# Two of four SwiGLU half-steps with seven half-size products per hidden tile in place of eight

## The chip, the cores and the metric

The kernel runs on one core of a Trainium2 chip, as one program. The time is the device time of the whole program in microseconds (us), the median of three runs. The engines are called TensorE (PE in the rows; PEld is its weight load), VectorE (DVE), ScalarE (ACT), GpSimd (POOL) and SyncE (SP, which only issues transfers here).

## The reference

Two layers run over a latent stream of 512 tokens and a context stream of 256 tokens, 1024 features wide, in float32. Each layer is a half-step, a mixer, and another half-step:

```python
x = x + 0.5 * mx[2] * _swiglu(_modulate(_rmsnorm(x, norm_g[l, 0]), mx[0], mx[1]),
                              ffn_w1[l, 0], ffn_w3[l, 0], ffn_w2[l, 0])
...
x = x + mx[5] * ox
...
x = x + 0.5 * mx[8] * _swiglu(_modulate(_rmsnorm(x, norm_g[l, 2]), mx[6], mx[7]),
                              ffn_w1[l, 1], ffn_w3[l, 1], ffn_w2[l, 1])

def _swiglu(h, w1, w3, w2):
    return (jax.nn.silu(h @ w1) * (h @ w3)) @ w2
```

`mx` is the latent stream's nine adaLN vectors, made from `silu(c) @ w_mod[l] + b_mod[l]`. The context stream takes the same steps with its own vectors; in the second layer it ends in the mixer, so that layer's second half-step is for the latent tokens alone. `w1` and `w3` are 1024 by 2816, `w2` is 2816 by 1024. The mixer is a projection `h @ w_in`, pooling, a retention with four heads, a convolution of 31 taps, and `@ w_out`. The output is the latent stream after a last norm.

## The kernel before

Features lie on the partitions and tokens along the free dimension. A float32 product is made exactly enough from three narrow ones: `split` (L150, L151) cuts a tile into a high part on ScalarE and a low part on VectorE, and `mm3` multiplies high by high, high by low and low by high into one bank of PSUM (L155 to L157).

`weights` gives the next 1024 columns of weights in the order of their use; it loads a block (L528) into one of six `raw` buffers, splits it, and works three blocks ahead (`LOOKAHEAD`). There are four buffers for high parts `wh` and four for low parts `wl`, so a block's split waits until TensorE has released the one four before it. All other activations lie in a pool of 66 slots of 128 by 512 values.

A half-step (`ffn`) goes through the 22 tiles of 128 hidden features in five pieces of 5, 5, 4, 4 and 4 (`PIECES`). For each tile, `up` multiplies eight tiles of `h` by `w1` and by `w3`, first for the 256 context tokens and then for the 512 latent ones; ScalarE takes the silu (L561), VectorE multiplies (L562), and `split` makes the parts of `g`. At the end of a piece come its products with `w2` (`down`), and VectorE adds them, times a gate, to the stream `x` in its slots (L599). In the last piece the squares of `x` are summed as well (L400, L401), a group's norm starts when its last tile is added, and `norm_tiles` (L474 to L480) makes the next `h`. In that last piece all the context's products come first, then all the latent ones, so one group's norm runs beside the other's products.

The adaLN vectors are made in the background by `mod_chunks`: loads of `w_mod`, multiplications on VectorE (L301, L303), and a small sum on TensorE (L319). What runs in the background is a generator; `spawn` and `poll` place its parts between TensorE's products by a clock that counts 0.000422 us for each column multiplied, and `drain` places all that is left at once:

```python
self.first = [self.spawn(self.mod_chunks(0, (2,), 4.0), 10.0)]
later = self.spawn(self.mod_chunks(0, range(3, 9), 6.0), 80.0)
...
    self.ffn(l, 0, h, both, both, both, done, begun)
    self.drain(later)
    self.decays()
```

While a mixer runs, `x` is kept in DRAM: `store_x` writes it after the norm, `load_x` reads it back before the products with `w_out`. The convolution's taps are a background task on VectorE (L745); `conv_norm`'s transposes (L845) come when all taps have been placed. The order on each engine comes from a scheduler, which takes of the ready instructions the one that comes first in the program.

## Time and profile before

| | |
|---|---|
| median of three runs | 2616.26 us (2614.4 to 2616.76) |
| span of the profiled execution | 2612.7 us |
| the median less that span | 3.6 us |
| TensorE, busy | 2580.8 us (99%) |
| VectorE, busy | 1624.4 us (62%) |
| ScalarE, busy | 722.5 us (28%) |
| DMA, mean | 104 GB/s |

The span is from the first to the last instruction of one profiled execution. For that execution there is no device time of its own, so what lies around the span is taken from the median of the runs. A busy time says how long an engine had an instruction in it; TensorE's matmuls overlap, so its share alone does not say that it is the limit.

### The profile page before, as it was taken

The page shows a single profiled execution, that of the slowest core. Times are in us where ns is not written, and L with a number is a line of the kernel's source. Part 1 is how long each engine was busy: PE and PEld are TensorE (multiplying, and loading weights), DVE is VectorE, ACT ScalarE, POOL GpSimd, SP SyncE. Part 2 cuts the span into 40 slices and gives each one's busy share as a digit, 9 for nine tenths or more (in the row PEclk, how much of TensorE's full clock was granted, in tenths as well). Part 3 has the DMA queues.
Part 4 walks back from the last instruction along what each step waited for, and adds up shares of the span by engine and source line. Part 5 has one row for each costly group of instructions (what it writes and reads, how often), then busy time and mean ns, then how long its engine had stood idle before and what let it go on. Part 6 is the DMA issues. An engine that isn't in the chain of part 4 may idle for free. (4 is left out here: it accounts for less than half of the span.)

```text
span 2612.7 us, 35462 instructions
## 1 busy us (share of the span) xinstructions
PE 2580.8 (99%) x14434; PEld 2241.5 (86%) x14434; DVE 1624.4 (62%) x3058; ACT 722.5 (28%) x1204; POOL 0.2 (0%) x4
## 2 busy tenths in 40 slices
PE   8999999999999999999999999999999999999998
PEld 4888888888898888888888888888888888888887
DVE  6776685747977777677333863645536697633335
ACT  3212112133334331212212412121223254422223
POOL 0000000000000000000000000000000000000000
PEclk9999999999999999999999999999999999999999
DMA  7343443322232134354211241433212332233331
GB/s 279 115 146 113 145 153 104 113 85 87 85 97 81 57 105 151 96 158 126 72 61 57 85 134 57 136 105 97 81 58 98 97 109 81 74 106 111 96 96 35
DMA packets 88003, 270.82 MB, mean 104 GB/s; under 512 B 10272, under 2 KB 12832, under 8 KB 87840
## 3 DMA queue, kind: packets, MB, share of 16 engines
q1 hardware_dynamic: 84768, 264.36, 32.1%
q10 hardware_dynamic: 3072, 4.20, 0.6%
q8 instruction: 113, 1.85, 0.3%
q14 instruction: 50, 0.41, 0.0%
HBM read 256.98 MB, written 7.34 MB: 101 GB/s over the span
## 5 line engine op out<-in xcount | busy, mean ns | idle before, releaser
L155 PE MATMUL up<-h,wh 128*128 128x512 f32 (+1 forms) x2496 | 852.1, 343 | 3.4 <-ACT h L476 1.7
L156 PE MATMUL up<-h,wh 128*128 128x512 f32 (+1 forms) x2496 | 853.0, 342 | 0.4 <-DVE h L478 0.2
L157 PE MATMUL up<-h,wl 128*128 128x512 f32 (+1 forms) x2496 | 849.9, 342 | 0.1
L150 ACT CAST wh<-raw 128x1024 fp32r<-128x1024 f32 (+1 forms) x348 | 344.0, 993 | 1261.7 <-PE down L156 442.2
L151 DVE TENSOR_TENSOR wl<-raw,wh 128x1024 fp32r<-128x1024 f32 (+1 forms) x348 | 398.2, 1148 | 333.1 <-ACT wh L150 318.2
L155 PEld LDWEIGHTS up<-h,wh 128*128 128x128 f32 x2496 | 472.2, 190 | 59.4 <-ACT h L476 2.0
L156 PEld LDWEIGHTS up<-h,wh 128*128 128x128 f32 x2496 | 473.0, 190 | 55.9 <-DVE h L478 1.0
L157 PEld LDWEIGHTS up<-h,wl 128*128 128x128 f32 x2496 | 472.3, 189 | 54.5 <-DVE wl L151 0.3
L155 PE MATMUL down<-g,wh 128*128 128x512 f32 (+1 forms) x1264 | 430.9, 341 | 0.0
L156 PE MATMUL down<-g,wh 128*128 128x512 f32 (+1 forms) x1264 | 430.3, 341 | 0.0
L157 PE MATMUL down<-g,wl 128*128 128x512 f32 (+1 forms) x1264 | 429.0, 339 | 0.0
L303 DVE SCALAR_TENSOR_TENSOR macc<-wm,sc,macc 128x512 f32<-128x512 f32 x462 | 319.0, 745 | 9.8 <-DMA wm<-in_w_mod_dram 9.6
L562 DVE TENSOR_TENSOR silu<-silu,up 128x512 f32<-128x512 f32 (+1 forms) x156 | 88.3, 566 | 341.1 <-PE up L157 340.7
L155 PEld LDWEIGHTS down<-g,wh 128*128 128x128 f32 x1264 | 239.7, 190 | 27.5 <-ACT g L150 0.2
L156 PEld LDWEIGHTS down<-g,wh 128*128 128x128 f32 x1264 | 239.8, 190 | 26.8 <-DVE g L151 0.6
L157 PEld LDWEIGHTS down<-g,wl 128*128 128x128 f32 x1264 | 239.3, 189 | 27.1
L599 DVE SCALAR_TENSOR_TENSOR x<-down,gate,x 128x256 f32<-128x256 f32 (+1 forms) x288 | 177.7, 621 | 136.3 <-PE down L157 134.4
L150 ACT CAST g<-silu 128x512 fp32r<-128x512 f32 (+1 forms) x156 | 81.8, 525 | 210.5 <-DVE silu L562 210.5
L745 DVE SCALAR_TENSOR_TENSOR conv<-z,dwh,conv 128x512 f32<-128x512 f32 (+1 forms) x180 | 109.8, 656 | 1.6
L151 DVE TENSOR_TENSOR g<-silu,g 128x512 fp32r<-128x512 f32 (+1 forms) x156 | 88.6, 568 | 23.7 <-ACT g L150 23.6
L561 ACT ACTIVATE silu<-up 128x512 f32<-128x512 f32 (+1 forms) x156 | 77.3, 496 | 87.0 <-PE up L157 86.7
L476 ACT ACTIVATE h<-ht,mod 128x256 fp32r<-128x256 f32 (+1 forms) x96 | 56.3, 597 | 81.5 <-DVE ht L474 81.4
(175 smaller groups left out, 2268.4 us busy)
## 6 DMA issues: line engine op xcount, KB each, us to landing
raw<-in_w_dram SPq DMA_DIRECT2D x224, 512.0 KB, 3.7
wm<-in_w_mod_dram SPq DMA_DIRECT2D x128, 512.0 KB, 3.9
raw<-in_w_dram SPq DMA_DIRECT2D x64, 320.0 KB, 3.0
raw<-in_w_feat_dram SPq DMA_DIRECT2D x36, 512.0 KB, 3.6
wm<-in_w_mod_dram SPq DMA_DIRECT2D x32, 256.0 KB, 6.0
raw<-in_w_out_dram SPq DMA_DIRECT2D x16, 512.0 KB, 4.8
xkept<-x SPq DMA_DIRECT2D x20, 256.0 KB, 2.5
x<-xkept SPq DMA_DIRECT2D x20, 256.0 KB, 6.0
```

Source lines behind the costliest of these rows:

```text
L150: self.nc.scalar.copy(hi, src)
L151: self.nc.vector.tensor_sub(lo, src, hi.bitcast(F32))
L155: nc.tensor.matmul(out, wh, xh, start=start, stop=False)
L156: nc.tensor.matmul(out, wh, xl, start=False, stop=False)
L157: nc.tensor.matmul(out, wl, xh, start=False, stop=stop)
L303: self.nc.vector.scalar_tensor_tensor(acc[v], raw, s, acc[v], op0=ALU.mult, op1=ALU.add)
L476: nc.scalar.activation(hi, t, AF.Identity, bias=sh)
L561: nc.scalar.activation(t, ps[f, 0], AF.Silu)
L562: nc.vector.tensor_mul(t, t, ps[f, 1])
L599: nc.vector.scalar_tensor_tensor(xd, ps, self.gate(l, idx, grp[0], dt), xd, op0=ALU.mult, op1=ALU.add)
L745: nc.vector.scalar_tensor_tensor(acc, src, w, acc, op0=ALU.mult, op1=ALU.add)
```

## The change

In the second half-step of the first layer and the first of the second layer (`HALVED`), the products of `h` with `w1` and `w3` are made by Strassen's scheme in Winograd's form. The 768 tokens are two halves of 384 (latent tokens 0 to 383; then latent 384 to 511 and the context), the 1024 features two halves of 512, and `w1` and `w3` of a hidden tile are the two halves of the output. Seven products of half size take the place of eight; sums and differences of the weights' halves are made for each tile on VectorE (`blocks`), those of `h` once for a half-step (`differences`, `first_difference`). The first two hidden tiles are still made the old way while the differences are made.

These half-steps go in eleven pieces of two hidden tiles. What a piece adds to the stream is no longer added on VectorE: ScalarE scales it into a slot and GpSimd issues a transfer that adds it to the stream in DRAM (`add_kept`); the stream is read back in the last tile. The first half of the products with `w_out` is added the same way in both mixers.

Besides: `PIECES` is 4, 4, 4, 4, 4, 2 in all half-steps; `h` lies in 16 rows of 768 tokens, and the other slots are 45; `raw` has five buffers; the first three adaLN vectors of the second layer are made in the first half-step and not in the second; two kinds of tiles of the mixer use other pools.

```diff
-PIECES = (5, 5, 4, 4, 4)
+PIECES = (4, 4, 4, 4, 4, 2)
...
+HALVED = ((0, 1), (1, 0))
+HK, HN, SUB = KD // 2, NT // 2, 2
+PARKED = ((0, 1), (1, 1), (0, 2), (1, 0))
...
-        self.spool = ctx.enter_context(tc.tile_pool(name="slots", bufs=66))
+        self.spool = ctx.enter_context(tc.tile_pool(name="slots", bufs=45))
+        self.rpool = ctx.enter_context(tc.tile_pool(name="rows", bufs=2 * KD))
...
+    def row(self, s, dt=F32):
+        return self.rpool.tile([P, NT], dt, tag="row", name=self.name(s))
...
+    def add_kept(self, dt, grp, ps, gate):
+        st, t0, n = grp
+        part = self.slot("xpart")[:, :n]
+        self.nc.scalar.activation(part, ps, AF.Copy, scale=gate)
+        c0 = dt * LEN[st] + t0
+        self.nc.gpsimd.dma_start(self.kept[st][:, c0 : c0 + n], part, accum_op=ALU.add)
...
-    def mod_chunks(self, l, js, pace):
...
+    def mod_chunks(self, ljs, pace):
+        nc = self.nc
+        for l, j in ljs:
...
-        if idx == 1:
-            if l < DEPTH - 1 or grp[0] == LAT:
+        if (l, idx) in PARKED:
+            if idx != 1 or l < DEPTH - 1 or grp[0] == LAT:
                 self.store_x(grp[0])
...
-        return self.wpool.tile([P, 1024], F32, tag="raw", name=self.name("raw"), bufs=6)[:, :n]
+        return self.wpool.tile([P, 1024], F32, tag="raw", name=self.name("raw"), bufs=5)[:, :n]
...
+        def halved(l, s):
+            f0 = 0
+            for npc in PIECES:
+                w2 = ins["w2"][l, s, :, f0 * D : (f0 + npc) * D].rearrange("p (d f n) -> p d f n", d=KD, f=npc)
+                for a in range(0, npc, SUB):
+                    for f in range(f0 + a, f0 + a + SUB):
+                        both = [ins["w13"][l, s, f, :, m * 1024 : (m + 1) * 1024] for m in range(2)]
+                        if f < NFIRST:
+                            yield from both
+                        else:
+                            yield both
+                    for d in range(0, KD, 4):
+                        yield w2[:, d : d + 4, a : a + SUB]
+                f0 += npc
...
+    def fetch(self, src):
+        raws = []
+        for a in src if isinstance(src, list) else [src]:
+            n = a.shape[-1] if len(a.shape) == 2 else 1024
+            raws.append(self.raw(n))
+            to = raws[-1] if len(a.shape) == 2 else raws[-1].rearrange("p (d f n) -> p d f n", d=4, f=SUB)
+            self.nc.sync.dma_start(to, a)
+        return raws
...
+        order = self.weight_order()
+        src = next(order)
+        raws = None
+        while src is not None:
+            if raws is None:
+                raws = self.fetch(src)
+            after = next(order, None)
+            early = None
+            if not isinstance(src, list):
+                if isinstance(after, list):
+                    early = self.fetch(after)
+                self.parts(raws[0])
+                yield
+            else:
+                w1, w3 = raws
+                half = slice(0, 512), slice(512, 1024)
+                b, c = self.raw(1024), self.raw(1024)
+                nc.vector.tensor_sub(b[:, half[0]], w1[:, half[0]], w3[:, half[0]])
+                nc.vector.tensor_add(c[:, half[0]], w3[:, half[0]], w3[:, half[1]])
+                self.parts(w1)
+                yield
+                nc.vector.tensor_sub(b[:, half[1]], c[:, half[0]], w1[:, half[0]])
+                self.parts(b)
+                early = self.fetch(after) if after is not None else None
+                yield
+                nc.vector.tensor_sub(c[:, half[1]], w1[:, half[1]], b[:, half[1]])
+                self.parts(c)
+                yield
+                self.parts(w3[:, half[1]])
+                yield
+            src, raws = after, early
...
+    def prepare(self, n):
+        while self.plan and len(self.ahead) < n:
+            if next(self.plan, self) is self:
+                self.plan = None
...
+    def sums(self, h, kt):
+        t = []
+        for k in (kt, kt + HK):
+            for c in (slice(0, HN), slice(HN, NT)):
+                t.append(self.slot("half")[:, :HN])
+                self.nc.vector.tensor_add(t[-1], h[0][k][:, c].bitcast(F32), h[1][k][:, c].bitcast(F32))
+        return t
...
+    def differences(self, h, T):
+        nc = self.nc
+        for kt in range(HK):
+            b11, b12, b21, b22 = self.sums(h, kt)
+            nc.vector.tensor_sub(b11, b12, b11)
+            nc.vector.tensor_sub(b12, b22, b12)
+            nc.vector.tensor_sub(b22, b22, b11)
+            nc.vector.tensor_sub(b21, b21, b22)
+            for i, t in ((3, b12), (2, b22), (4, b21)):
+                for p in range(2):
+                    T[i][p][kt] = self.slot("t", F32R)[:, :HN]
+                self.split(t, T[i][0][kt], T[i][1][kt])
+            yield 3.6
...
+    def first_difference(self, h):
+        nc = self.nc
+        a, b = slice(0, HN), slice(HN, NT)
+        for kt in range(HK):
+            t, u = (self.slot("half")[:, :HN] for _ in range(2))
+            for v, c in ((t, b), (u, a)):
+                nc.vector.tensor_add(v, h[0][kt][:, c].bitcast(F32), h[1][kt][:, c].bitcast(F32))
+            nc.vector.tensor_sub(t, t, u)
+            self.split(t, h[0][kt][:, b], h[1][kt][:, b])
...
+    def up_halved(self, f, h, T, g, load=None):
+        nc = self.nc
+        self.prepare(4)
+        wa, wb, wc, wd = (self.ahead.pop(0) for _ in range(4))
+        a, b = slice(0, HN), slice(HN, NT)
...
+            for kt in range(HK):
+                c = slice(half * 512 + kt * P, half * 512 + (kt + 1) * P)
+                self.mm3(ps, w[0][:, c], w[1][:, c], tile(0, kt), tile(1, kt), start and kt == 0, kt == HK - 1, True)
+            self.poll()
...
+        pa, pd = (self.psum("up")[:, :HN] for _ in range(2))
+        product(pa, wa, 0, of_h(0, a), True)
+        c11 = copied(pa)
+        product(pd, wb, 0, of_t(3), True)
+        p7 = copied(pd)
+        product(pa, wb, 1, of_t(2), False)
+        c21 = copied(pa)
+        if load:
+            load()
+        pb = self.psum("up")[:, :HN]
+        product(pb, wa, 1, of_h(HK, a), True)
+        nc.vector.tensor_add(c11, pb, c11)
+        nc.scalar.activation(c11, c11, AF.Silu)
+        self.prepare(1)
+        product(pa, wc, 0, of_h(0, b), False)
+        c22 = copied(pa)
+        self.prepare(2)
+        product(pd, wd, 0, of_t(4), False)
+        nc.vector.tensor_add(c21, pd, c21)
+        nc.vector.tensor_mul(c11, c11, c21)
+        grp = (LAT, 0, HN)
+        self.split(c11, self.put(g, 0, f, grp, "g0"), self.put(g, 1, f, grp, "g1"))
+        nc.vector.tensor_add(c22, c22, p7)
+        product(pa, wc, 1, of_h(HK, b), False)
+        self.prepare(3)
+        nc.scalar.activation(p7, pa, AF.Silu)
+        nc.vector.tensor_mul(p7, p7, c22)
+        for grp, c in (((CTX, 0, LC), slice(HN - LC, HN)), ((LAT, HN, LX - HN), slice(0, LX - HN))):
+            self.split(p7[:, c], self.put(g, 0, f, grp, "g0"), self.put(g, 1, f, grp, "g1"))
+        self.prepare(4)
...
+    def ffn_halved(self, l, s, h, starts, grps, ends, done):
+        nc = self.nc
+        idx = 2 * s
+        accs = {}
+        T = {i: [[None] * HK for _ in range(2)] for i in (2, 3, 4)}
+        for f0 in range(0, NF, SUB):
+            g = self.empty()
+            last = f0 == NF - SUB
+            def load():
+                for st in (CTX, LAT):
+                    self.load_x(st, self.kept[st])
+            if f0 == 0:
+                ws = {f: self.w13() for f in range(SUB)}
+                for grp in starts:
+                    self.need(grp)
+                    if grp is starts[-1]:
+                        task = self.spawn(self.differences(h, T), 1.0)
+                    self.up(ws, range(SUB), h, g, grp)
+                self.drain(task)
+                self.first_difference(h)
+            else:
+                for f in range(SUB):
+                    self.up_halved(f, h, T, g, load if last and f == SUB - 1 else None)
+            w2 = []
+            def down(dt, grp, ps, fs):
+                self.products([(ps, w2[dt // 4], dt % 4 * SUB * P + fs[0] * P)], g, grp, fs, fs[0] == 0, fs[-1] == SUB - 1)
+            if last:
+                w2 = [self.weights() for _ in range(2)]
+                for grp in ends:
+                    for dt in range(KD):
+                        ps = self.psum("down")[:, : grp[2]]
+                        down(dt, grp, ps, range(SUB))
+                        xd = self.xs(dt, grp)
+                        nc.vector.scalar_tensor_tensor(xd, ps, self.gate(l, idx, grp[0], dt), xd, op0=ALU.mult, op1=ALU.add)
+                        self.square(dt, grp, accs)
+                    done(grp, accs)
+            else:
+                for d in range(0, KD, 2):
+                    if d % 4 == 0:
+                        w2.append(self.weights())
+                    these = [(dt, grp, self.psum("down")[:, : grp[2]]) for dt in (d, d + 1) for grp in grps]
+                    for fs in ((0,), (1,)):
+                        for dt, grp, ps in these:
+                            down(dt, grp, ps, fs)
+                    for dt, grp, ps in these:
+                        self.add_kept(dt, grp, ps, self.gate(l, idx, grp[0], dt))
...
+                    if t % 4 == 0:
+                        two = self.wide("zn")
+                    zn.append(two[:, t % 4 * 256 : t % 4 * 256 + 512])
                 nc.scalar.activation(zn[t // 2][:, (t % 2) * 256 : (t % 2 + 1) * 256], zt, AF.Identity, scale=rs[:, t : t + 1], bias=nb[:, t : t + 1])
...
+            def spare(s):
+                return self.slot(s) if chunks[0] < nc_ctx else self.row(s)[:, :512]
...
-        for st in streams:
-            self.x[st] = [None] * (KD if st == LAT else KD // 2)
-            self.load_x(st, self.kept[st])
...
+            if i == 0:
+                return self.add_kept(dt, grp, ps, self.gate(l, 1, grp[0], dt))
...
+        for st in streams:
+            self.load_x(st, self.kept[st])
...
-        self.first = [self.spawn(self.mod_chunks(0, (2,), 4.0), 10.0)]
-        later = self.spawn(self.mod_chunks(0, range(3, 9), 6.0), 80.0)
+        self.first = [self.spawn(self.mod_chunks([(0, 2)], 4.0), 10.0)]
+        later = self.spawn(self.mod_chunks([(0, j) for j in range(3, 9)] + [(1, j) for j in range(3)], 6.0), 80.0)
...
-                later = self.spawn(self.mod_chunks(l, range(5, 9), 11.2), 20.0)
-                self.ffn(l, 0, h, both, both, both, done)
+                later = self.spawn(self.mod_chunks([(l, j) for j in range(5, 9)], 11.2), 20.0)
+                self.ffn_halved(l, 0, h, both, both, both, done)
...
-                later = self.spawn(self.mod_chunks(l + 1, range(5), 6.84), 20.0)
+                later = self.spawn(self.mod_chunks([(l + 1, j) for j in range(3, 5)], 6.84), 40.0)
...
-            self.ffn(l, 1, h2, cuts, grps, cuts, done)
+            (self.ffn if last else self.ffn_halved)(l, 1, h2, cuts, grps, cuts, done)
```

## Rows read from the trace of the kernel before

**Rows 1.** The page, part 1: engine, busy us (share of the span), instructions.

```profile
span 2612.7 us, 35462 instructions
...
PE 2580.8 (99%) x14434; PEld 2241.5 (86%) x14434; DVE 1624.4 (62%) x3058; ACT 722.5 (28%) x1204; POOL 0.2 (0%) x4
```

**Rows 2.** Waits of PE: engine, line and releaser: us in total, times, longest us.

```profile
PE modf L280 <- DMA wm<-in_w_mod_dram: 8.5, 2, 5.5
...
PE cb L862 <- ACT y L967: 1.9, 1, 1.9
...
PE o L953 <- DVE sc L935: 1.6, 2, 1.4
```

**Rows 3.** Windows of whole tiles: stretch, us, busy us (instructions) of each engine, PEclk, DMA.

```profile
2400.75:2444.27 43.52, 43.52 (x193) 36.04 (x192) 14.42 (x15) 12.05 (x15) 0.00 (x0) 1.00 0.36 108
294.76:361.68 66.92, 66.92 (x388) 59.28 (x387) 41.87 (x72) 15.25 (x23) 0.00 (x0) 1.00 0.39 118
361.68:395.12 33.44, 33.44 (x194) 29.51 (x193) 29.41 (x46) 4.78 (x6) 0.00 (x0) 1.00 0.53 174
```

**Rows 4.** Groups by form, VectorE: busy us, mean ns, idle before and releaser.

```profile
L151 DVE TENSOR_TENSOR wl<-raw,wh 128x1024 fp32r<-128x1024 f32 x284 | 345.8, 1223 | 293.6 <-ACT wh L150 278.9
L303 DVE SCALAR_TENSOR_TENSOR macc<-wm,sc,macc 128x512 f32<-128x512 f32 x462 | 319.0, 745 | 9.8 <-DMA wm<-in_w_mod_dram 9.6
...
L562 DVE TENSOR_TENSOR silu<-silu,up 128x512 f32<-128x512 f32 x86 | 59.0, 687 | 223.1 <-PE up L157 222.8
...
L562 DVE TENSOR_TENSOR silu<-silu,up 128x256 f32<-128x256 f32 x70 | 29.2, 418 | 118.0 <-PE up L157 117.9
```

**Rows 5.** Groups by form, ScalarE.

```profile
L150 ACT CAST wh<-raw 128x1024 fp32r<-128x1024 f32 x284 | 297.2, 1052 | 1007.4 <-PE down L156 329.0 <-PE up L156 300.2 <-issue 243.6
...
L561 ACT ACTIVATE silu<-up 128x512 f32<-128x512 f32 x86 | 50.7, 589 | 0.3 <-DMA raw<-in_w_dram 0.3
...
L150 ACT CAST g<-silu 128x256 fp32r<-128x256 f32 x70 | 28.3, 406 | 193.7 <-DVE silu L562 193.7
...
L561 ACT ACTIVATE silu<-up 128x256 f32<-128x256 f32 x70 | 26.7, 382 | 86.7 <-PE up L157 86.7
```

**Rows 6.** Timeline of VectorE where a piece's products with w2 begin.

```profile
562.80 0.69 DVE L562 TENSOR_TENSOR silu<-silu,up 128x512 f32<-128x512 f32 x1 [3.38 <-PE up L157]
563.62 1.23 DVE L151 TENSOR_TENSOR wl<-raw,wh 128x1024 fp32r<-128x1024 f32 x1
564.77 0.68 DVE L151 TENSOR_TENSOR g<-silu,g 128x512 fp32r<-128x512 f32 x1
```

**Rows 7.** Windows of a half-step's end: stretch, us, busy us (instructions), PEclk, DMA.

```profile
1418.40:1457.00 38.60, 38.60 (x235) 34.58 (x234) 32.13 (x66) 17.45 (x30) 0.00 (x0) 1.00 0.18 57
1457.00:1463.50 6.50, 6.50 (x52) 6.02 (x52) 2.72 (x16) 0.00 (x0) 0.00 (x0) 1.00 0.20 72
```

**Rows 8.** TensorE's sums for the adaLN vectors in the first half-step, by tile.

```profile
L319 PE MATMUL mods<-mrow,cs x6: 217/245/273, 399.8 to 527.6; 128*128 128x64 f32 x6
```

**Rows 9.** Timeline of VectorE at the last tap of the convolution.

```profile
739.39 0.74 DVE L745 SCALAR_TENSOR_TENSOR conv<-z,dwh,conv 128x512 f32<-128x512 f32 x1
```

**Rows 10.** Timeline of TensorE at the transposes that read the taps' result.

```profile
775.97 0.82 PE L845 MATMUL cz<-cs,conv 128*128 128x128 f32 x6
```

**Rows 11.** Windows after TensorE's waits: stretch, us, busy us (instructions), PEclk, DMA.

```profile
20.20:23.50 3.30, 3.30 (x4) 0.46 (x5) 1.39 (x2) 0.39 (x1) 0.00 (x0) 0.50 1.05 389
...
794.90:798.30 3.40, 3.40 (x18) 3.35 (x17) 1.18 (x2) 3.37 (x9) 0.00 (x0) 0.51 0.42 149
...
817.30:822.00 4.70, 2.68 (x12) 1.76 (x12) 4.68 (x8) 0.00 (x0) 0.00 (x0) 1.00 0.57 224
```

**Rows 12.** The page, part 6: transfers, KB each, median us to landing.

```profile
raw<-in_w_dram SPq DMA_DIRECT2D x224, 512.0 KB, 3.7
...
xkept<-x SPq DMA_DIRECT2D x20, 256.0 KB, 2.5
x<-xkept SPq DMA_DIRECT2D x20, 256.0 KB, 6.0
```

64 lines of the change are left out of this document (39 added, 25 removed).

## The prediction, made before the changed kernel ran

> **What bounds the kernel now.** I read the page's busy times first: TensorE has an instruction in it for 99% of the span, VectorE for 62%, ScalarE for 28% [rows 1]. Overlapping matmuls make that 99% no proof, so the next view is what TensorE waited for. The thirteen rows of that view add to about 24 us of 2612.7; the longest are for the first loads, and later only single ones of 1.9 and 1.4 us [rows 2]. The windows of whole hidden tiles then show a steady pace without gaps: four tiles of `up` take 66.92 us and their `down` 33.44 us, where VectorE is busy from a third to nearly nine tenths [rows 3]. So TensorE's columns set the time, and the other engines have just enough room to stay hidden. A change that takes columns away is paid in full, less whatever it uncovers.
>
> **What is removed.** A tile of a halved step has 7 x 4 x 3 = 84 matmuls of 384 columns in place of 48 of 512 and 48 of 256. Latent tokens alone show the wide ones: 43.52 / 192 = 0.2267 us each. The rest of a mixed window, (66.92 - 43.52) / 192 = 0.1219 us, is the narrow one [rows 3]. The trace has no matmul of 384 columns; halfway between is 0.1743. A tile then goes from 16.73 to 84 x 0.1743 = 14.64 us, 2.09 less, and 20 tiles in each of two half-steps give **83.6 us**. If the price per column were that of the wide form (0.170 a matmul) it would be 98, if that of the narrow one (0.183), 55. I take the middle, because the two prices lie on a line with a small constant part. `down` has as many matmuls as before.
>
> **The ends of half-steps.** The last piece shrinks from four tiles to two in all four half-steps. Its `down` is what covers the adding to `x`, the squares and the next norm. In such an end VectorE is busy 32.1 of 38.6 us, and 6.5 us more pass from the last square to the latent norm's first tile [rows 7]. VectorE's work there does not depend on the number of tiles. TensorE will have only 16.7 us of `down` and 96 x 0.122 = 11.7 us of the context's next products, 28.4 in all, against 32.1 + 6.5 = 38.6. That loses 10 us an end, or 4 if the five weight splits in it (1.22 each [rows 4]) move behind; 15 with the stream read back late. I take 7 for each of three ends, 21, and 4 for the fourth, where only latent tokens are left and nothing follows (0 to 10).
>
> **The starts of halved steps.** `differences` is 4 x 11 operations on VectorE of 384 columns. Between 0.418 for 256 and 0.687 for 512 [rows 4] that is 0.553 each, 24.3 us. The latent norm in front is 16 operations of 0.745 (the price of the same operation in the adaLN sums [rows 4]), 11.9 us; weights and the context's `g` add 4.1. That is 40.3 us while TensorE has 96 x 0.2267 = 21.8 us of the first two tiles' latent products. If the latent `g` goes behind all of it, `down` waits 18.5 us. If `g` (2.7) goes first, the differences are ready at 43.0 and TensorE needs them at 21.8 + 16.7 + 2.1 = 40.6, a wait of 2.4. The program order, by which the scheduler chooses, speaks for the long one; the differences' own pauses for ScalarE's copies let `g` in between. I take 7 for each, **14** for both. `first_difference` (16 operations, 8.8 us) is needed 25 us after the old products end and fits behind.
>
> **The boundary from `up` to `down`,** ten in each half-step. The last product's chain is silu 0.49, multiply 0.55, copy of the context's part 0.41, subtraction 0.42 (between the rows' widths, or at 256 [rows 4, 5]), 1.9 us. `down` begins with the first hidden tile for four groups, 6 x (0.227 + 0.122) = 2.1 us of cover, so with hand-overs the wait is 0.2. But a weight block's cast (1.05) and split (1.22) become ready at the same moment, as TensorE releases a `wh` buffer. In the trace such a split does stand between the multiply and the last subtraction of `g` [rows 6]; there 3.5 us of `down` covered it. With both in front the wait is 2.4. I take 0.7, since only the tile's last block lies in the way: 20 x 0.7 = **14** (4 to 48).
>
> **ScalarE and VectorE in between.** A piece of two tiles lasts 2 x 14.64 + 16.72 = 46.0 us on TensorE. ScalarE has nine blocks of casts at most (9.5), eight copies and four silus (5.8), the parts of `g` and 16 scalings, near 26 us; VectorE has 8 sums (5.5), the splits (11) and the tile's own work (8), near 25, and loses the 16 additions. With the adaLN work it is below 40. Each product leaves 2.1 us for the copy of the bank that it leaves. These edits cost nothing as long as the cover holds; without it, it is the boundary's price again.
>
> **The adding in DRAM.** Before, GpSimd issues nothing like it, so the price is bounded by the stream's own transfers, 2.5 us to land a store and 6.0 a load [rows 12]. A piece makes 16 of them. They touch different columns; only if each waited for the one before does the latency count, and 46.0 / 16 = 2.87 us is the point from which that decides. I take nothing for it. The Trainium skill, page "DMA: Bandwidth & Descriptors", section "Anatomy of one DMA — SWDGE (gpsimd) path", fits such a transfer as 2.0 us plus its bytes over 436e3. By that page, as an estimate, 16 transfers one after another are about 39 us, still under the piece, and the term stays zero; no run here shows it yet.
>
> **The stream's return.** In the last tile the loads are issued four products (8.4 us) and the context's `down` ahead of the latent additions; one load lands in 6.0 us [rows 12]. In the mixers the same wait falls behind the first half of `w_out`. I take 3 for all of it (0 to 20).
>
> **The moved adaLN vectors.** In the first half-step one vector takes (527.6 - 399.8) / 2 = 63.9 us of pace [rows 8]. With three more the last would be done at 527.6 + 3 x 63.9 = 719, but the step ends near 562.6 + 33.4 = 596 [rows 3, 6]. The `drain` then places two whole vectors ahead of the mixer: 64 operations of 0.745 and eight folds, 53 us of VectorE, and 16 loads on SyncE's queue, ahead of the weights' splits. What waits is the convolution's taps. Their last is at 740.1 and the transposes that read it at 776.0, so 36 us are free [rows 9, 10], and weights are three blocks ahead. I take 5 (0 to 25). The second half-step loses that work, which was hidden.
>
> **The clock.** After the waits of 5.5 and 1.9 us the granted clock was 0.50 and 0.51 for 3.4 us, that is 1.2 in place of 2.4 GHz; after the one of 1.4 us it stayed at 1.00 [rows 2, 11]. Each longer wait costs 1.7 us more. Three ends and two starts: 8.5 (5 to 40).
>
> **Sum.** 83.6 - 21 - 4 - 14 - 14 - 0 - 3 - 5 - 8.5 = 14.1 us faster. The profiled execution, with its span of 2612.7 us and the 3.6 us around it, stands at the median of the runs, 2616.3; so 2602.
>
> **Rivals.**
> *The boundary decides.* At each of the 20 boundaries cast and split go first and TensorE waits 2.4 us. For it: rows 6 show that order. Against: only one block is ready there. The price is 20 x 1.7 = 34 us on top, 2636; and since 2.4 is longer than the 1.9 us after which the clock fell, up to 34 more, 2670. The forecast turns into a loss from 1.4 us a boundary on.
> *Starts and dump at their upper ends.* `g` stands behind all differences (18.5 us twice) and the adaLN dump reaches TensorE (25): 2602 + 23 + 20 = 2645. For it: program order. Against: the 36 us of slack and the pauses.
> *Nearly all stays hidden.* Ends 4, starts 2.4, boundaries 0.2 and three falls of the clock: 12 + 5 + 4 + 5 = 26 lost, 2558.
> *The columns do not fall as counted.* A matmul of 384 columns costs 0.183: 55 gained, 2631. Against: the narrow form's constant part.
> *The additions go one by one.* At 6.0 us each, 96 us a piece against 46: 20 x 50 = 1000 us more. Against: different columns, and stores land in 2.5.
>
> **How the numbers follow.** Within 0.2% (5 us) a measurement of this kernel can't tell a change from none. The forecast's case has 0.45, with a range of its own from 2585 to 2618: 0.33 of it faster, 0.10 the same, 0.02 slower. Nearly all hidden 0.17 (faster); the boundary 0.18, starts and dump 0.11, columns 0.05, one by one 0.04 (slower). That makes 0.50 faster, 0.10 the same and 0.40 slower. The range from 2556 to 2650 takes in the hidden case, the boundary at its lower price, and the columns and starts; it leaves out the boundary with the clock, part of the hidden case, and the additions one by one.
>
> **What would show it.** Right: 84 matmuls at 0.174 a tile; gaps on TensorE of 5 to 10 us where a half-step ends and a latent `g` or the differences are awaited; under 1 us between `up` and `down`; no wait on GpSimd's transfers. Wrong: equal gaps of over 1.9 us at every boundary with the clock at 0.5 behind them, ScalarE waiting for slots, or a gap near 640 to 780 us. The sum of small waits is the weakest part: three of its terms have upper ends that each eat the gain.

## The result, and the profile after

The changed kernel takes **2716.63 us**, the median of four runs (2712.72 to 2721.88), against 2615.76 us before in the same session: **1.0387 times, interval 1.0373 to 1.0402, slower by 101 us**. Forecast were 2602 us and a range from 2556 to 2650. The profiled execution has a span of 2715.9 us.

The page of the kernel after, busy us and share of the span by engine, and its transfers:

```profile
span 2715.9 us, 36761 instructions
...
PE 2533.0 (93%) x13906; PEld 2247.8 (83%) x13906; DVE 1835.3 (68%) x3430; ACT 1050.3 (39%) x1840; POOL 304.4 (11%) x348
...
L231 POOL DMA_DIRECT2D xkept<-xpart x344 | 304.2, 1420 | 1995.4 <-ACT xpart L229 1957.7
...
raw<-in_w_dram SPq DMA_DIRECT2D x260, 512.0 KB, 3.7
...
xkept<-xpart POOLq DMA_DIRECT2D x176, 256.0 KB, 8.5
xkept<-xpart POOLq DMA_DIRECT2D x168, 128.0 KB, 8.0
```

TensorE was in work for 99% of the span before [rows 1] and is for 93% now. It has less to do and waits more. GpSimd is the new engine at work. Its row reads 344 instructions of 1.42 us each on the mean, but they overlap: 304.2 us for all of them is 0.88 us for each accumulating transfer.

The waits of TensorE in the kernel after (us in total, times, longest us):

```profile
PE mods L337 <- DVE mrow L330: 53.9, 2, 27.4
PE down L164 <- ACT g L159: 47.0, 7, 21.9
PE ms L427 <- DVE acc L419: 24.0, 8, 8.8
PE rstd L443 <- DVE diag L434: 21.9, 6, 8.8
PE modf L298 <- DMA wm<-in_w_mod_dram: 8.7, 2, 5.6
...
PE up L164 <- ACT half L765: 2.8, 2, 2.0
```

Before, the longest row of this view was the 8.5 us for the first loads [rows 2]. It is fifth now. Four kinds of waits stand above it: for the small sums of the adaLN vectors, for the gated units at the start of a halved half-step, and for the mean square and its root at the ends. No row names a transfer to DRAM.

Windows of the kernel after (stretch, us, busy us and instructions of PE, PEld, DVE, ACT and POOL, granted clock, DMA share, GB/s):

```profile
596.50:682.60 86.10, 11.02 (x28) 7.44 (x29) 80.06 (x166) 14.92 (x26) 0.00 (x0) 0.54 0.36 122
627.50:682.60 55.10, 1.18 (x5) 0.94 (x5) 52.17 (x97) 5.77 (x9) 0.00 (x0) 0.50 0.29 98
1015.00:1052.80 37.80, 20.27 (x98) 16.98 (x97) 33.54 (x60) 17.80 (x33) 10.32 (x12) 0.73 0.33 70
1575.10:1618.60 43.50, 19.83 (x98) 16.58 (x97) 39.97 (x71) 17.38 (x33) 8.28 (x10) 0.73 0.34 85
1202.27:1231.57 29.30, 29.30 (x171) 29.30 (x170) 16.47 (x24) 14.77 (x26) 2.64 (x3) 1.00 0.59 142
1231.41:1248.46 17.05, 17.05 (x98) 14.62 (x98) 7.09 (x11) 10.73 (x20) 11.38 (x13) 1.00 0.78 130
1506.59:1575.22 68.63, 60.45 (x318) 51.19 (x317) 58.30 (x128) 29.42 (x53) 0.00 (x0) 0.93 0.26 96
2061.40:2130.59 69.19, 60.96 (x317) 51.56 (x317) 46.10 (x103) 26.62 (x52) 0.00 (x0) 0.93 0.28 98
```

The fifth and sixth rows are one steady piece of a halved half-step: two tiles in 29.30 us, 14.65 each where 14.64 was forecast, then their `down`, with no gap between. The scheme itself does what the sum said. The first row is the 86 us from the time at which the first mixer began before (596.5) to its first product now. TensorE has 11 us of work in it, among them the last of the half-step's `down`, and VectorE 80. The second row is its last 55 us, at a granted clock of 0.50. The third and fourth are the first `down` of the two halved half-steps: 37.8 and 43.5 us for what takes 17.05 in the sixth row. The last two are ends of halved half-steps with the first two tiles or `kq` products after them. TensorE's work there is 17.05 for `down`, some 2.3 for the last product of `up`, and 66.92 / 2 = 33.46 for what follows [rows 3], together 52.8; 15.8 and 16.4 us are lost. Some 2.5 us of each are the norm's own small matmuls, which the kernel before has at its ends too.

By stages, from one stage's first product to the next one's (before, then after):

```
start of the first mixer (point in time)      596.8 -> 682.6   +85.8
first mixer                                   301.7 -> 297.3    -4.4
halved half-step of the first layer           554.2 -> 552.4    -1.9
halved half-step of the second layer          553.9 -> 555.7    +1.7
second mixer                                  224.5 -> 238.9   +14.4
last half-step                                381.5 -> 389.1    +7.6
```

The first line gives points in time, the others durations. The sum is 103.2 us, the difference of the spans. The halved half-steps came out even: some 84 us of columns went, in the main, into their starts and ends. The loss lies elsewhere, most of it at one place.

**The place.** Timeline of TensorE in the kernel after, between the first half-step and the first mixer (start, us, line, operation, idle before and its releaser):

```profile
619.40 2.08 PE L427 MATMUL ms<-ones,acc 128*128 128x128 f32 x8 [8.82 <-DVE acc L419]
625.48 2.08 PE L443 MATMUL rstd<-diag,ones 128*128 128x512 f32 x2 [4.00 <-DVE diag L434]
654.09 0.69 PE L337 MATMUL mods<-mrow,cs 128*128 128x64 f32 x2 [26.54 <-DVE mrow L330]
682.16 0.69 PE L337 MATMUL mods<-mrow,cs 128*128 128x64 f32 x2 [27.38 <-DVE mrow L330]
682.61 0.56 PE L164 MATMUL cv<-h,wh 128*128 128x256 f32 x1
```

And VectorE's timeline in the same stretch:

```profile
621.25 1.22 DVE L160 TENSOR_TENSOR wl<-raw,wh 128x1024 fp32r<-128x1024 f32 x1
...
636.84 0.75 DVE L508 SCALAR_TENSOR_TENSOR h<-ht,mod,h 128x512 fp32r<-128x512 f32 x1
637.50 0.70 DVE L329 STREAM_TRANSPOSE mturn<-macc 128x512 f32<-128x512 f32 x1
638.13 0.71 DVE L510 SCALAR_TENSOR_TENSOR h<-ht,mod,h 128x512 fp32r<-128x512 f32 x1
...
655.86 4.07 DVE L321 SCALAR_TENSOR_TENSOR macc<-wm,sc,macc 128x512 f32<-128x512 f32 x6
...
660.88 5.39 DVE L321 SCALAR_TENSOR_TENSOR macc<-wm,sc,macc 128x512 f32<-128x512 f32 x8 [0.81 <-DMA wm<-in_w_mod_dram]
```

The mixer's input `h` is ready at 638.8, and TensorE starts on it at 682.6. In between stand two small sums of 0.69 us each (two matmuls apiece). They sum the two adaLN vectors that `drain` placed ahead of the mixer, and they are ahead of the mixer's products in TensorE's own queue. The first waits for the rest of the norm, until 638.8, and then for the 16 multiplications and the folds that its vector still lacks; the second waits for all 32 multiplications and the folds of its own. The weights were not what the mixer waited for: their last split is the one at 621.25, none follows before 682.6, and `cv` starts right behind the second sum. That the sums hold the mixer is read from this order; no run moves the two sums alone, for e1 and e2 move the multiplications with them.

### The profile page after: what moved, and what is told of

The parts are those of the page before. It is cut to its first block, busy times and chain, and to the rows that moved or that the text cites. A ratio compares the mean times of both kernels' runs of the same rounds, so it can differ in the third digit from the quotient of the medians.

```text
span 2715.9 us, 36761 instructions
## 1 busy us (share of the span) xinstructions
PE 2533.0 (93%) x13906; PEld 2247.8 (83%) x13906; DVE 1835.3 (68%) x3430; ACT 1050.3 (39%) x1840; POOL 304.4 (11%) x348
## 4 chain that ended last, share of the span: by engine, by line
PE 44%; issue 8%; DVE 3%; DMA 1%; ACT 1%; POOL 0%; ACTq 0%; DVEq 0%; POOLq 0%; SPq 0%
PE up L164 9%; PE up L165 9%; PE up L166 9%; PE down L164 5%; PE down L165 5%; PE down L166 5%; DVE acc L419 1%; DVE wl L160 0%; DMA xkept<-xpart 0%; DMA x<-xkept 0%; DVE x L836 0%; DVE macc L321 0%; PE ms L427 0%; PE rstd L443 0%; ACT wh L159 0%
## 5 line engine op out<-in xcount | busy, mean ns | idle before, releaser
L164 PE MATMUL up<-h,wh 128*128 128x512 f32 (+2 forms) x1856 | 636.2, 345 | 4.3 <-ACT h L506 3.9
L165 PE MATMUL up<-h,wh 128*128 128x512 f32 (+2 forms) x1856 | 637.7, 344 | 0.5 <-DVE h L508 0.3
L166 PE MATMUL up<-h,wl 128*128 128x512 f32 (+2 forms) x1856 | 636.3, 344 | 0.1
L231 POOL DMA_DIRECT2D xkept<-xpart x344 | 304.2, 1420 | 1995.4 <-ACT xpart L229 1957.7
L164 PE MATMUL down<-g,wh 128*128 128x256 f32 (+1 forms) x1248 | 427.7, 351 | 51.5 <-ACT g L159 47.0
L165 PE MATMUL down<-g,wh 128*128 128x256 f32 (+1 forms) x1248 | 433.2, 348 | 0.0
L166 PE MATMUL down<-g,wl 128*128 128x256 f32 (+1 forms) x1248 | 429.4, 346 | 0.0
L164 PEld LDWEIGHTS up<-h,wh 128*128 128x128 f32 x1856 | 350.5, 189 | 36.9 <-ACT h L506 5.9
L165 PEld LDWEIGHTS up<-h,wh 128*128 128x128 f32 x1856 | 351.3, 189 | 31.6 <-DVE h L508 1.8
L166 PEld LDWEIGHTS up<-h,wl 128*128 128x128 f32 x1856 | 351.2, 189 | 29.1 <-DVE wl L160 0.3
L164 PEld LDWEIGHTS down<-g,wh 128*128 128x128 f32 x1248 | 236.5, 192 | 87.3 <-ACT g L159 53.9
L165 PEld LDWEIGHTS down<-g,wh 128*128 128x128 f32 x1248 | 240.1, 193 | 29.3 <-DVE g L160 1.9
L229 ACT ACTIVATE xpart<-down,gate 128x256 f32<-128x256 f32 x320 | 173.3, 583 | 88.3 <-PE down L166 87.3
L164 PE MATMUL up<-t,wh 128*128 128x384 f32 x480 | 160.6, 335 | 2.8 <-ACT half L765 2.8
L166 PE MATMUL up<-t,wl 128*128 128x384 f32 x480 | 160.4, 334 | 0.0
L165 PE MATMUL up<-t,wh 128*128 128x384 f32 x480 | 160.4, 334 | 0.0
```

Source lines behind the costliest of these rows:

```text
L164: nc.tensor.matmul(out, wh, xh, start=start, stop=False, skip_group_check=shared)
L165: nc.tensor.matmul(out, wh, xl, start=False, stop=False, skip_group_check=shared)
L166: nc.tensor.matmul(out, wl, xh, start=False, stop=stop, skip_group_check=shared)
L229: self.nc.scalar.activation(part, ps, AF.Copy, scale=gate)
L231: self.nc.gpsimd.dma_start(self.kept[st][:, c0 : c0 + n], part, accum_op=ALU.add)
```

## The experiments

Each run stands beside the kernel before on the same chip (2614.5 to 2615.4 us).

**e1: the vectors inside their half-steps.** One vector of the second layer stays in the first half-step, four go to the second.

```diff
-        later = self.spawn(self.mod_chunks([(0, j) for j in range(3, 9)] + [(1, j) for j in range(3)], 6.0), 80.0)
+        later = self.spawn(self.mod_chunks([(0, j) for j in range(3, 9)] + [(1, j) for j in range(1)], 6.0), 80.0)
...
-                later = self.spawn(self.mod_chunks([(l + 1, j) for j in range(3, 5)], 6.84), 40.0)
+                later = self.spawn(self.mod_chunks([(l + 1, j) for j in range(1, 5)], 6.84), 40.0)
```

> The changed kernel with one adaLN vector of the second layer moved to the first half-step in place of three; the other two stay in the second half-step. Theory A (TensorE's queue holds the vectors' small sums ahead of the mixer, and waits for VectorE): the stretch from the first half-step's last latent product to the mixer's first product, 72 us in the changed kernel, shrinks to under 10, and the time falls by 75 to 85, to about 2636. Rival B (VectorE's work is what counts, and it only moves): two vectors more in the second half-step stretch its pieces by most of what is saved, 50 us or so, and the time stays above 2680.

Measured: 2657.99 us, 1.016 [1.0145, 1.0176], 59 under the kernel after. The gap ahead of the first mixer lost some 77 us: both waits for `mods` are gone, and waits of 3.83, 1.04 and 1.60 us stay. But the first halved half-step grew from 552.4 to 565.0 us, with new waits of up to 5.0 us while the four vectors ran in it. So the vectors were the largest loss, and they are not free where they go instead.

**e2: the vectors alone, in the kernel before.** Nine vectors in the first half-step and two in the second, as the change places them; nothing else changed.

```diff
-        later = self.spawn(self.mod_chunks(0, range(3, 9), 6.0), 80.0)
+        later = self.spawn(self.mod_chunks([(0, j) for j in range(3, 9)] + [(1, j) for j in range(3)], 6.0), 80.0)
...
-                later = self.spawn(self.mod_chunks(l + 1, range(5), 6.84), 20.0)
+                later = self.spawn(self.mod_chunks([(l + 1, j) for j in range(3, 5)], 6.84), 40.0)
```

> The kernel before with this part of the change alone: three adaLN vectors of the second layer in the first half-step, two in the second. Theory A: the two small sums in TensorE's queue hold the mixer back as they do in the changed kernel, +75 to +85, about 2695. What was forecast (the surplus lies beside the mixer's work, and 36 us are free at the taps): +5, at most +25, so 2621 to 2641.

Measured: 2692.47 us, 1.0293 [1.0276, 1.031], **+78 us**. TensorE's waits in this run:

```profile
PE mods L319 <- DVE mrow L312: 54.8, 2, 27.6
PE ms L409 <- DVE acc L401: 12.6, 3, 9.2
PE rstd L425 <- DVE diag L416: 10.7, 3, 7.8
```

This one edit, without a line of Strassen's scheme, gives the kernel before the same two waits for `mods` and most of the loss.

**e3: the short end alone, in the kernel before.**

```diff
-PIECES = (5, 5, 4, 4, 4)
+PIECES = (4, 4, 4, 4, 4, 2)
```

> The kernel before with pieces of 4, 4, 4, 4, 4 and 2 tiles alone. Theory A (an end of a half-step takes VectorE's time however short the products with w2 are; the ends of the changed kernel's two halved steps take 69 us as they did before, with 16.7 us less work for TensorE): +14 to +16 for each of three ends and +8 for the last, +50 to +56, about 2669. What was forecast: +7 each and +4, so 2641. Rival B (the long ends of the changed kernel come from reading the stream back): +5 or less here, where the stream stays on the chip.

Measured: 2659.91 us, 1.0171 [1.0156, 1.0186], **+45 us** for four ends, where the prediction had 25. The waits are small ones for `rstd` (18.7 us in eight) and `ms` (8.3 in six), and the clock that falls behind them.

**e4: the gated units ahead of the differences.**

```diff
                 for grp in starts:
                     self.need(grp)
-                    if grp is starts[-1]:
-                        task = self.spawn(self.differences(h, T), 1.0)
                     self.up(ws, range(SUB), h, g, grp)
+                task = self.spawn(self.differences(h, T), 1.0)
```

> The changed kernel with the differences placed behind the gated units of the first two tiles in the program; nothing else moves. Theory A (program order alone makes the latent silu and its parts wait on ScalarE and VectorE behind the differences): the waits of 17.5 and 21.9 us before the first products with w2 fall under 3 each, at most 5 us come back at the second piece, and with the low clock behind them the time falls by 35 to 45, to about 2676. Rival B (VectorE has 40 us to do in any order): the wait moves to the first halved tile, which needs the differences, and the time stays within 12 us of 2717.

Measured: 2736.35 us, 1.0464, 20 us over the kernel after; both theories fell. The wait of 17.5 us became 3.4, and a new one of 29.3 stood inside the same `down`. ScalarE's timeline of this run shows what it waited for:

```profile
1043.12 0.51 ACT L159 CAST t<-half 128x384 fp32r<-128x384 f32 x1 [0.50 <-DVE half L726]
1049.85 0.51 ACT L159 CAST t<-half 128x384 fp32r<-128x384 f32 x1 [6.22 <-DVE half L724]
...
1055.40 0.51 ACT L159 CAST h<-half 128x384 fp32r<-128x384 f32 x1 [2.63 <-DVE half L740]
1057.27 0.51 ACT L159 CAST h<-half 128x384 fp32r<-128x384 f32 x1 [1.36 <-DVE half L740]
1057.69 0.47 ACT L229 ACTIVATE xpart<-down,gate 128x256 f32<-128x256 f32 x1
```

The copies of the differences wait for VectorE, and behind them in ScalarE's queue stand the scalings that empty the PSUM tiles of the first `down`. In the kernel after, the latent `silu` stands there. The last product of `up` ended at 1015.2, and its `silu` came 16 us later, behind the copies:

```profile
1029.56 1.10 ACT L159 CAST t<-half 128x384 fp32r<-128x384 f32 x2 [4.25 <-DVE half L724]
1031.16 0.51 ACT L159 CAST t<-half 128x384 fp32r<-128x384 f32 x1 [0.50 <-DVE half L726]
1031.58 0.59 ACT L653 ACTIVATE silu<-up 128x512 f32<-128x512 f32 x1
```

The block of differences holds whatever comes next on ScalarE. Its order does not help; it has to be taken apart.

**e5: the differences thinly.** Four hidden tiles the old way instead of two; the differences behind the first two tiles' `g`, with pauses inside each of the four steps.

```diff
             b11, b12, b21, b22 = self.sums(h, kt)
+            yield 3.6
...
             nc.vector.tensor_sub(b21, b21, b22)
+            yield 3.6
...
-            if f0 == 0:
+            if f0 < 2 * SUB:
...
+                if f0 == 0:
+                    task = self.spawn(self.differences(h, T), 1.0)
+                else:
+                    self.drain(task)
+                    self.first_difference(h)
```

> The kernel after, with four hidden tiles instead of two made the old way at the start of both halved half-steps; the differences start behind the second tile's gated units and are laid out in twelve pieces over the first products down and the next two tiles up. The two extra tiles cost 2 x 2 x 2.09 = 8.4 us. Theory A (the start's waits of 17.5 and 21.9 us and the low clock behind them come from the differences standing in one block ahead of other work in the in-order queues of VectorE and ScalarE): the first products down fall from 37.9 and 43.7 to about 17.2 us each, -47, together -39: about 2678 us. Rival B (VectorE and ScalarE have no 30 us to give within the start, wherever the work is put): the wait comes back at the second products down or the first halved tile and the time stays within 10 us of 2717.

Measured: 2713.94 us, 1.038, 3 under the kernel after; 39 were expected. At the starts themselves it worked: the first `down` took 21.7 us in both half-steps instead of 37.9 and 43.7, the second 26.6 and 24.8. The gain was lost elsewhere. In the second halved half-step two pairs of tiles, without a gap in the kernel after, now took 39.1 and 35.5 us instead of 29.3.

**e6, e7: slower vectors, and both edits.** The four vectors of e1 at 12.0 us a piece from 70 us on instead of 6.84 from 40; then the same with e5's start.

> The kernel after, with one vector of the second layer in the first half-step and four in the second, as in the run with the vectors in time, but the four paced at 12.0 us a piece from 70 us on instead of 6.84 from 40. Theory A (four vectors cost some 15 us in the second half-step because their pieces crowd the start of it): 2640 to 2648 us against 2658. Rival B (they cost by their number, wherever they are put): 2654 to 2662.

> Both edits together. Theory A (two separate costs): the two gains add up, 2678 - 2717 + 2643 = about 2604 us, the first time under the kernel before (2615). Rival B (both draw on the same free VectorE time, so one takes what the other gives): 2630 us or more.

Measured: 2654.52 us (1.0147) and 2678.37 us (1.0238). Theory A missed in both; the times are those that rival B gave (2654 to 2662, and over 2630). At the slower pace the last of the four vectors was not done when its half-step ended, and e2's wait came back there in small: 13.28 us for `mods`, behind 11.37 for `ms`. The thin start, which should have added its gain, made e6's kernel 24 us slower: again stretched tiles, now in both half-steps (36.1, 38.4, 39.5, 35.5 us).

**e8: long ends.** e7 with the last `down` of each half-step from four hidden tiles.

```diff
-PIECES = (4, 4, 4, 4, 4, 2)
+PIECES = (4, 2, 4, 4, 4, 4)
...
-        for f0 in range(0, NF, SUB):
+        for f0 in (*range(0, NF - 4, SUB), NF - 4):
...
-            last = f0 == NF - SUB
+            last = f0 == NF - 4
```

> Both edits, and the last products down of every half-step from four hidden tiles instead of two (pieces of 4, 2, 4, 4, 4, 4; the two halved half-steps put their last two pairs together). Theory A (each of the two short ends inside the halved half-steps costs about 16 us, the one ahead of the first mixer and the tail about 8 each): 45 us under the run without it, about 2555 to 2565 us. Rival B (the ends' waits come from the norm's chain alone and not from how much TensorE has to do beside it): within 15 us of the run without it.

Measured: 2636.43 us, 1.0078, 42 under e7, near theory A's 45. The stretched tiles stayed. VectorE's timeline at one of them, in e8:

```profile
1728.90 0.69 DVE L610 TENSOR_TENSOR raw<-raw,raw 128x512 f32<-128x512 f32 x1
1733.86 2.74 DVE L321 SCALAR_TENSOR_TENSOR macc<-wm,sc,macc 128x512 f32<-128x512 f32 x4 [4.27 <-DMA wm<-in_w_mod_dram]
1742.05 1.41 DVE L321 SCALAR_TENSOR_TENSOR macc<-wm,sc,macc 128x512 f32<-128x512 f32 x2 [5.45 <-DMA wm<-in_w_mod_dram]
1743.38 1.22 DVE L160 TENSOR_TENSOR wl<-raw,wh 128x1024 fp32r<-128x1024 f32 x1
1744.62 0.56 DVE L785 TENSOR_TENSOR half<-up,half 128x384 f32<-128x384 f32 x1
```

and the window over the transfers just ahead of it:

```profile
1716.00:1738.00 22.00, 22.00 (x129) 20.72 (x129) 12.38 (x25) 12.05 (x22) 14.06 (x16) 1.00 1.06 186
```

VectorE, busy for 12 of those 22 us, stands before the adaLN multiplications until their weights land. The sum `half` at 1744.62 stands behind them. ScalarE's `silu` waits for that sum, and behind the `silu` stands the copy that empties the bank for TensorE's next product:

```profile
1745.22 0.52 ACT L786 ACTIVATE half<-half 128x384 f32<-128x384 f32 x1 [9.64 <-DVE half L785]
1745.64 0.46 ACT L771 COPY half<-up 128x384 f32<-128x384 f32 x1
...
PE up L164 <- ACT half L771: 7.3, 1, 7.3
```

The last row is TensorE's wait between 1725 and 1750. In the 22 us of the window GpSimd issues the 16 accumulating transfers of a piece, and the DMA engines are full (share 1.06), with the loads beside them.

**e9 and e10: whose loads are late.** e9 loads each adaLN piece's weights one piece ahead of its multiplications, and paces the four vectors at 9.5 us from 40 us on, so that they end in time. e10 is e8 without the accumulating transfers of the halved half-steps.

```diff
...
+        coming = load()
...
-                    raw = self.wide("wm").rearrange("p (k n) -> p k n", k=2)
-                    nc.sync.dma_start(raw, self.ins["w_mod"][l, j, half, kk])
+                    raw, coming = coming, load() if at else None
...
```

```diff
-        self.nc.gpsimd.dma_start(self.kept[st][:, c0 : c0 + n], part, accum_op=ALU.add)
+        if add:
+            self.nc.gpsimd.dma_start(self.kept[st][:, c0 : c0 + n], part, accum_op=ALU.add)
```

> The run with thin starts, slow vectors and long ends (2636 us), with each adaLN piece's weights loaded one piece before VectorE's multiplications of them are put in its queue, and the second half-step's four vectors at 9.5 us from 40 us on, so that they end inside it. In that run four halved tiles or pairs took 7.1, 6.0, 10.2 and 5.6 us more than their 29.3 or 56.6, and two more some 1 us each, while VectorE stood before macc<-wm for the DMA; the end of the second half-step waited 4.25, 3.14 and 13.28 us and ran 27 us at half clock (about 37 in all). Theory A (VectorE's in-order queue stands for loads that land late, and the late sums hold TensorE's queue): both go, 2636 - 32 - 37 = about 2567 us. Rival B (VectorE simply has too much to do): the waits move elsewhere, 2610 or more.

> The same run (2636 us) without the accumulating transfers of the two halved half-steps: ScalarE still scales the products down, nothing is added in DRAM, so the output lacks those sums. Theory A (sixteen accumulating transfers in a burst fill the DMA engines for some 20 us, and the adaLN weights issued in that time land late): the four stretched places go back to 29.3 and 56.6 us, the end's late vectors stay: 2636 - 32 = about 2604 us. Rival B (the weights are late by their place in the queue of SyncE, behind blocks that wait for a free buffer): 2630 to 2636 us, the macc<-wm waits stay.

e10: 2606.36 us, 0.9965 [0.9952, 0.9978], 30 under e8 where theory A said 32; the four stretched places took 29.28, 56.70, 29.41 and 30.18 us. The same stretch in e10, over the same products:

```profile
1702.00:1724.00 22.00, 22.00 (x128) 20.73 (x128) 16.44 (x31) 12.73 (x23) 0.00 (x0) 1.00 0.34 100
```

The DMA share is a third of e8's. So the accumulating transfers do cost, by way of other loads. e9: 2602.85 us, 0.9952 [0.9937, 0.9967]; 2567 was expected. The end of the first halved half-step became some 31 us shorter, where 37 were forecast, and that half-step's stretched tiles went too, though its second `down` grew to 31.5 us. In the second half-step they stayed (38.2 and 37.1 us): one piece ahead was not early enough, and VectorE still waited 3.4 and 6.3 us there for the weights.

**e12: the second mixer's read-back.** e9 with the second pair of tiles going tile by tile, and the second mixer's stream read back before its first output products and added to in SBUF, as in the kernel before.

```diff
...
         load(0)
+        if not full:
+            self.load_x(LAT, self.kept[LAT])
...
-            if i == 0:
+            if i == 0 and full:
                 return self.add_kept(dt, grp, ps, self.gate(l, 1, grp[0], dt))
```

> The run with loads ahead, with two more edits that stand in different places: the second pair of tiles in each halved half-step goes tile by tile, so that the products down find their first gated units ready (a wait of 3.38 + 1.75 us each goes to about 2: -3 each); and the second mixer reads the stream back before its first output products and adds in SBUF, as the kernel before does. Theory A (the second mixer's waits of 3.6 to 4.0 us for the mean square and what follows come from reading the stream back after its DRAM additions): mixer 2 falls from 232 to about 225 us; with the pairs, 13 us under the run with loads ahead. Rival B (those waits come from VectorE and ScalarE alone): within 7 us of it.

Measured: 2576.99 us, 0.9854 [0.9838, 0.9871], 26 under e9, twice what was expected. The second mixer went from 231.9 to 226.3 us, its waits for the mean square gone. The rest came from the halved half-steps, whose stretched tiles shrank to one of 38.7 us and a few of 1 to 3; that part was not forecast.

**e13, e14, e15: one thing each against e12.** e13 loads the adaLN weights two pieces ahead, with a third buffer. Its two slots come off the 45. e14 is e12 without e5's and e12's edits of the start, e15 is e12 without e8's edits of the ends.

```diff
-        return self.wpool.tile([P, 1024], F32, tag="wm", name=self.name(s), bufs=2)
+        return self.wpool.tile([P, 1024], F32, tag="wm", name=self.name(s), bufs=3)
...
-        coming = load()
+        coming = [load(), load()]
```

> The run with the stream read early in the second mixer (2577 us), with the adaLN weights loaded two pieces ahead instead of one (a third buffer; two slots of 45 given up for it). In that run six halved tiles or pairs still took 1.0, 9.4, 0.6, 2.8, 0.3 and 1.9 us more than 29.3 or 56.6, 16 us in all. Theory A (what is left is VectorE standing for adaLN weights that land behind the accumulating transfers): most of it goes, 2562 to 2568 us. Rival B (loads two ahead meet the same burst of transfers, or the two slots are missed): 2573 us or more.

> The run with the stream read early in the second mixer (2577 us), with the start of the change put back: two hidden tiles the old way, the differences in one block. The thin starts gained only 3 us of 39 forecast when they were tried first, where late adaLN loads stretched other tiles. Theory A (the start's block costs what the trace showed, and the first try lost the gain to those loads): the first four tiles and their products down take 125 us in each halved half-step instead of 111.5 and 110.2, +28 in all: about 2605 us. Rival B (the thin start gains nothing, its extra tiles cost what the waits did): 2571 to 2583 us.

> The run with the stream read early in the second mixer (2577 us), with the short ends put back: every half-step's last products down from two hidden tiles (pieces 4, 4, 4, 4, 4, 2). Theory A (a short end leaves the norm's chain uncovered, as much as the step from the seventh to the eighth run gave: 42 us over five places): about 2619 us. Rival B (part of those 42 was late vectors and clock, which are gone here): 2590 to 2605 us.

Measured: e13 **2565.07 us, 0.9807 [0.9793, 0.9822]**, 12 under e12; e14 2614.51 us (2606.93 to 2616.53), +37.5; e15 2622.29 us (2614.37 to 2625.7), +45. Theory A held in all three, in e14 with 10 us more than it said. e14's first four tiles took 120.4 and 125.2 us against 111.5 and 110.2, so 24 of its 37.5 us lie at the starts and the rest in tiles stretched by late loads. TensorE's waits in e13:

```profile
PE modf L298 <- DMA wm<-in_w_mod_dram: 9.2, 2, 6.2
PE down L164 <- ACT g L159: 7.3, 3, 2.8
PE down L164 <- ACT xpart L229: 5.4, 3, 2.8
PE rstd L452 <- DVE diag L443: 3.6, 3, 2.7
```

The wait for the first loads is on top again, as before [rows 2]. With the scheme kept and its surroundings put right, the kernel is 50 us (1.9%) faster than before, and 152 us faster than the change.

## Why the prediction was wrong, point by point

**The columns (right).** 14.64 us a tile were forecast from the middle of two prices; 29.30 / 2 = 14.65 came. The 83.6 us are there.

**The moved adaLN vectors (the step that failed).** I wrote that the dump costs VectorE 53 us, and that "what waits is the convolution's taps", of which 36 us were free; 5 us, at most 25. The size of the dump was about right: VectorE worked 52.2 of the 55.1 us in which the two waits lie, 11 of them still on the norm. The waiter was wrong. The vectors' small sums are TensorE instructions, placed ahead of the mixer, so TensorE itself stood for 53.9 us; the squares and the root waited longer behind the multiplications as well. The granted clock was 0.54 on the mean over the 86 us, and 0.50, which is 1.2 GHz, over the last 55. e2 prices the edit at 78 us in the kernel before; 2716.6 - 78 = 2639 would have been inside the range.

**The starts (direction right, size wrong).** Forecast 14 for both, 18.5 each as the upper end. The waits were 17.53 and 21.92 us, so the upper end came true, and the clock fell behind them: the windows give 37.8 + 43.5 - 2 x 17.05 = 47.2 us. e14, which has the old starts, has waits of 17.53 and 21.93 us there again, and first `down`s of 36.9 and 43.5 us. It is only 37.5 us slower than e12, of which 24 lie at the starts, because e12's own starts are not free: two more tiles the old way in each half-step cost it 8.4 us in all, and its first two `down`s some 17. Where I took the differences' pauses for ScalarE's copies as what lets `g` in between, ScalarE's timelines in the changed kernel and in e4 show them to be what keeps it out: ScalarE's queue stands in those pauses, and `silu` stands in that queue.

**The ends (direction right, size wrong).** 25 for four, 10 us an end before what might move behind. e3 and e15, one on either side of the change, both give 45 us. In the changed kernel the two halved ends lost 15.8 and 16.4 us, or 13.3 and 13.9 without the norm's own matmuls. That is near the 15 that I had for an end with the stream read back late, but by luck as far as the runs show: no wait of TensorE there names the read-back. Its waits, some 8 us in each end, are for the gated units, the mean square, its root and the first `h`, and the rest goes with the low clock behind them; in the kernel before, where nothing is read back late, e3's ends cost 11 us each.

**The boundary from `up` to `down` (too dear).** 14 us forecast, none to be seen in the steady pieces; there are single waits of 4.1 and 1.0 us at boundaries, and 2.8 us inside `up`, early in the first halved half-step, while adaLN vectors ran beside. No run shows that the vectors caused them. The rival in which the boundary decides is out.

**The adding in DRAM (right here, and incomplete).** No wait of TensorE in the changed kernel names it. But the landing was bounded by plain transfers of 2.5 and 6.0 us, and it took 8.5 and 8.0. The Trainium skill's page "DMA: Bandwidth & Descriptors", section "Anatomy of one DMA — SWDGE (gpsimd) path", gives 2.0 us and the bytes over 436e3, as an estimate 2.6 us for 256 KB; the measurement decides, and 8.5 us is three times that, with up to 16 issued in a burst. I looked for a queue on these transfers alone, and not for who else needs the DMA engines while they are full, for 22 us in the window of e8: with adaLN loads in that time it was 30 us (e8 against e10), nearly all of it in the four stretched places.

**The stream's return.** 3 us forecast; in the second mixer alone 5.6 (e9 to e12).

**The clock.** 8.5 us for five falls of 3.4 us. It stayed low for 55 us at one place, and at the two starts for some 6 us of work behind the wait: TensorE's work in the two first `down`s took 20.27 and 19.83 us instead of 17.05. Elsewhere it fell with the waits too, so it has no single price here. The prediction also read the waits of the kernel before too briefly: its last norm, at the end of the last half-step, has waits of 1.5 us for the mean square and 2.7 for the root, where it counted only "single ones of 1.9 and 1.4". And the stretch at a clock of 0.50 that it put behind the wait of 5.5 us stands behind one of 3.0.

**The sum again**, by these prices: -83.6 + 78 + 47 + 45 + 6 + 5 (the early boundaries) = +97, against +101 measured; 4 us stay open. The 78 and one of the two 45s were measured in the kernel before, one edit at a time, and that they add up in the changed kernel is an assumption. The rival with starts and dump at their upper ends was the right mechanism at two of three places, and by far too cheap. The others fell, "nearly all stays hidden" among them. What is still only argued is why one adaLN piece meets a burst of accumulating transfers and another does not: e5, e7 and e12 moved these waits without meaning to, and none of them was forecast.

## What to carry to other kernels

When work is moved to fill an engine's idle time, list every engine on which it leaves an instruction: a sum of 0.69 us placed ahead of the next stage holds the whole of TensorE until the slow engine is done. A block of work that alternates between two engines holds both queues for its full length; spread it in pieces that each find their operands ready. Transfers that nobody waits for are still to be priced by what they do to the loads beside them, and a gain that small waits can eat is to be forecast at their upper ends, not at the middle.

## What the runs showed of the hardware

- Sixteen accumulating transfers of 128 or 256 KB, issued by GpSimd within a piece, and the loads beside them kept the DMA engines full (share 1.06) for 22 us in e8. Each took 8.0 to 9.4 us to land there (medians of 8.0 and 8.5 us in the changed kernel), and GpSimd was busy for 304.2 / 344 = 0.88 us with each. Loads of 512 KB that landed in 3.6 us elsewhere in the changed kernel's profile took 7.3 us in such a stretch of e8.
- A matmul of 384 columns with its own weights costs 29.30 / 168 = 0.1744 us, on the line between 0.1219 (256) and 0.2267 (512).
- The granted clock was 0.50, that is 1.2 GHz, through the whole of a gap of 55 us, and 0.73 on average over a `down` that began with a wait of 17.5 us.
